# Normed x kept in DRAM, token-major operands copied once, bonus weights in the selector

## The chip, the cores and the metric

The kernel runs on one core of one Trainium2 chip. The metric is the device time of one execution in microseconds; for the kernel before, three runs gave a median of 797.93 us (796.2 to 800.12). A core has a matrix engine (PE), a vector engine (DVE), a scalar engine (ACT), a general engine (POOL) and an engine that issues most transfers (SP). PE writes into eight PSUM banks of 128 x 512 fp32; the other operands lie in SBUF.

## The reference

Two decoder layers over 512 tokens of width 1024. The change lies in layer 0, RWKV-7 time mixing:

```python
xn = rms_norm(h, norm_pre[0])
x_prev = pad(xn)[:, :-1]
xmix = xn + (x_prev - xn) * mu[c]          # one mix for each of r, k, v, g (and two more)
r, k, v, g = xmix[c] @ w_in[c]             # 1024 x 1024 each
decay = exp(-exp(-softplus(-w_pre) - 0.5)) # w_pre and a from two small products
kk = k * k_k / norm(k * k_k);  k = k * (1 + (a - 1) * k_a)
state = state * decay - (state @ kk) (kk * a)^T + v k^T;  y = state @ r      # over tokens
y = group_norm(y) * lnx_g + lnx_b
y = (y + sum(r * k * r_k, head) * v) * silu(g)
out = y @ w_out
```

Layer 1 is differential attention. Each layer ends with a gated embedding: p @ ple_w, gated by sigmoid(h @ ple_gate), normed and added.

## The kernel before, in words

All of layer 0 is built by about thirty Python generators, which a planner (`Streams`) runs against each other. Each yields the engine and an estimated duration of its next piece, waits for named events, or takes and frees buffers; the planner always records the piece that can start first by its estimates. So the order of every engine is a table that the planner makes from its estimated costs, and a changed cost, wait or buffer moves work far away. On the chip each engine goes through its order strictly, and an instruction that waits stops all behind it. SP's transfers are in one such queue.

Work is done in *dense groups*: three matmuls of 128 x 512 for one 128 x 128 block of weights, with operands split into a high and a low part (`mm3`, L285 to L287). `fill` (L907) runs the projections in the order r, k, v (first halves), r, k, v (second halves), the embedding's product `p` of layer 0, g, g, and the embedding of layer 1. Each half has 8 blocks of x times 4 output tiles, 32 groups. Its weights come through `w_load` (SP) and `w_split` (ACT, DVE, POOL), its operand, a mix of x with its neighbour token, through `mix` (L532). The first half of r, k and v forms the mixes (`mixed`, L512: ACT, DVE, ACT, DVE) and stores them in DRAM (mD, L529); the second half loads them again (L542). The mixes of g are formed ahead by `mix_ahead`, once the second half of k is done, and all halves of g load them.

Buffers are few: 43 ring slots of 4 KB per partition (R), 9 of 2 KB (H), and 8 PSUM banks (p), which projections and everything else share. xh, the normed and transposed x, holds four R slots until `mix_ahead` is done.

Between the dense groups runs the recurrence. `decay` (L740) forms decays and partial operands of one 128-wide tile from two small products (L749, L750). `k_evac` evacuates k and normalises it; its product r * k goes, scaled by r_k on ACT (L904), through `head_sums` with the selector `hsel` on PE (L824). `gram` (L984) forms products of keys within 128 tokens, `inverse` solves the triangular systems: a substitution on DVE, two sets of 64 small matmuls (L1087, L1101), and copies of small blocks. It begins with a load of identity blocks (L1025, `in_eye`), which ACT copies to PSUM (L1030). `operands` transposes keys into token-major form and copies them back into their place in four copies on ACT (L1152). `recur` goes through eight chunks of 64 tokens for each half of the heads: products with the Gram matrix (L1188), with the state (L1201), and the state's update (L1229 on PE, L1241 and L1244 on DVE). `finish` norms, adds the bonus, gates (L1310) and splits the result for the output projection (`layer_end`), whose groups follow `fill` directly. `pe_evac` copies the embedding's product to H on ACT (L1501) and SP stores it (peD, L1504); `v_evac` stores v (vcD, L664), and `operands` loads it (L1142).

## Time and profile before

| | |
|---|---|
| median of three runs | 797.93 us |
| profiled execution, its span | 797.09 us, 795.3 us |
| PE busy | 756.1 us (95%), 5016 matmuls |
| DVE, ACT, POOL busy | 589.8, 454.5, 201.9 us |
| mean granted clock of PE | 0.989 |
| moved by transfers | 148.79 MB, 187 GB/s |
| dense matmuls (L285 to L287) | 2400 |

In the prediction, a row of the page's fifth part or of a view by groups reads: line, engine, operation, output <- inputs, shapes, count | busy us, mean ns of one | idle us of the engine before them, and what ended it. A row of a timeline reads: start, length in us, engine, line, operation, count, and in brackets the idle time before it with its releaser. A row "PE p L749 <- ACT R L1115" tells how long the one waited for the other: total, times, longest. A row of a view by windows reads: window, its length, busy time and count of each engine (of PE alone where there is one), the granted clock, the share of the DMA engines, GB/s. A row of transfers ends with KB each and the median us from issue to landing.

### The profile page before, as it was taken

What the parts mean: (1) busy time and instruction counts of PE and PEld (TensorE: products, weight loads), DVE (VectorE), ACT (ScalarE), POOL (GpSimd) and SP (SyncE); (2) the same over time, 40 slices, a digit from 0 to 9 for tenths busy, and PEclk for the clock granted to TensorE, in tenths of its full rate; (3) what the DMA queues carried; (4) which work ended last, traced back from release to release, by engine and by line L of the source; (5) the groups of instructions that cost most, each with busy time, mean ns of one, the idle gap of its engine ahead of it and who ended that gap; (6) DMA issues with size and microseconds to landing.
All of it is one profiled execution on the core that took longest, in us unless ns stands there. A gap on an engine that the chain in (4) does not pass through costs nothing.

```text
span 795.3 us, 13941 instructions
## 1 busy us (share of the span) xinstructions
PE 756.1 (95%) x5016; PEld 605.1 (76%) x5016; DVE 589.8 (74%) x1360; ACT 454.5 (57%) x1078; POOL 201.9 (25%) x221
## 2 busy tenths in 40 slices
PE   6899999998999899999989999999999999999996
PEld 3576578875777677777778888887888888888884
DVE  2989999976798898998676685446874768835844
ACT  3779745688875446664444564333764566743431
POOL 2416615521451425666010010000000001100000
PEclk9999999998999899999999999999999999999998
DMA  8585669843684687463446444488943523314602
GB/s 325 197 285 196 245 225 290 298 147 105 209 286 171 217 301 258 145 228 105 133 166 247 133 146 135 172 309 226 312 158 92 159 53 121 117 43 159 259 6 106
DMA packets 66677, 148.79 MB, mean 187 GB/s; under 512 B 6576, under 2 KB 27312, under 8 KB 66608
## 3 DMA queue, kind: packets, MB, share of 16 engines
q1 hardware_dynamic: 43824, 112.25, 41.9%
q10 hardware_dynamic: 22784, 35.66, 13.1%
q8 instruction: 39, 0.64, 0.3%
q14 instruction: 30, 0.25, 0.1%
HBM read 110.13 MB, written 37.75 MB: 186 GB/s over the span
## 4 chain that ended last, share of the span: by engine, by line
PE 70%; DVE 8%; ACT 8%; DMA 8%; issue 2%; POOL 2%; SPq 1%; ACTq 0%; POOLq 0%; DVEq 0%
PE p L285 18%; PE p L287 18%; PE p L286 18%; PE p L1788 2%; PE p L984 2%; PE p L1188 2%; ACT R L270 1%; PE p L1753 1%; PE p L1752 1%; PE p L1201 1%; DMA R<-bD 1%; PE p L1779 1%; DMA RAW<-in_ple_w 1%; PE p L1410 1%; DMA R<-mD 1%
## 5 line engine op out<-in xcount | busy, mean ns | idle before, releaser
L285 PE MATMUL p<-R,R 128*128 128x512 f32 x800 | 326.4, 408 | 3.2 <-DVE R L270 1.7
L286 PE MATMUL p<-R,R 128*128 128x512 f32 x800 | 314.1, 393 | 3.8 <-DVE R L525 3.6
L287 PE MATMUL p<-R,R 128*128 128x512 f32 x800 | 314.4, 393 | 0.0
L285 PEld LDWEIGHTS p<-R,R 128*128 128x128 f32 x800 | 151.3, 189 | 37.1 <-DVE R L270 1.9
L287 PEld LDWEIGHTS p<-R,R 128*128 128x128 f32 x800 | 151.0, 189 | 33.2 <-DVE R L1318 0.4
L286 PEld LDWEIGHTS p<-R,R 128*128 128x128 f32 x800 | 151.5, 189 | 32.4 <-DVE R L525 4.9
L318 POOL TENSOR_TENSOR R<-RAW,R 128x512 fp32r<-128x512 f32 x59 | 78.6, 1339 | 163.3 <-ACT R L270 89.1
L270 ACT CAST R<-RAW 128x512 fp32r<-128x512 f32 x110 | 66.1, 619 | 26.7 <-DMA RAW<-in_w_g 10.0
L318 DVE TENSOR_TENSOR R<-RAW,R 128x512 fp32r<-128x512 f32 x81 | 56.8, 715 | 11.0 <-ACT R L270 10.2
L324 DVE SCALAR_TENSOR_TENSOR R<-RAW,vec,R 128x512 fp32r<-128x512 f32 x64 | 46.6, 748 | 13.9 <-ACT R L322 13.7
L322 ACT ACTIVATE R<-RAW,vec 128x512 fp32r<-128x512 f32 x64 | 44.6, 720 | 17.0 <-DMA RAW<-in_b_w_in 9.1
L1397 POOL TENSOR_TENSOR hr<-hm,half 128x1 f32<-128x1 f32 x16 | 10.4, 648 | 147.2 <-DVE hm L1395 147.2
L1757 DVE CUSTOM_DVE_ANT_0 p<-p,cmask 128x128 f32<-128x128 f32 (+3 forms) x64 | 30.3, 509 | 17.4 <-PE p L1753 17.3
L1764 ACT ACTIVATE H<-p,mx 128x128 f32<-128x128 f32 (+3 forms) x64 | 33.3, 526 | 15.7 <-DVE mx L1761 14.1
L281 POOL TENSOR_TENSOR orr<-orm,half 128x4 f32<-128x4 f32 x8 | 8.4, 1055 | 123.3 <-DVE orm L279 93.3
L1054 DVE TENSOR_TENSOR p<-p,H 128x126 f32<-128x126 f32 (+22 forms) x124 | 32.6, 263 | 4.3
L1051 DVE TENSOR_TENSOR H<-p,R 128x126 f32<-128x126 f32 (+22 forms) x124 | 30.5, 246 | 1.1
L1534 DVE SCALAR_TENSOR_TENSOR R<-H,R 128x512 f32<-128x512 f32 x16 | 11.1, 691 | 24.5 <-ACT H L1527 23.1
L1527 ACT ACTIVATE H<-p 128x512 f32<-128x512 f32 x16 | 9.5, 596 | 31.6 <-PE p L287 31.6
L521 DVE SCALAR_TENSOR_TENSOR p<-R,vec,p 128x511 f32<-128x511 f32 x32 | 23.5, 747 | 5.4 <-ACT p L519 5.3
L519 ACT ACTIVATE p<-R,omm 128x512 f32<-128x512 f32 x32 | 22.0, 695 | 5.0 <-DVE R L525 3.7
L1788 PEld LDWEIGHTS p<-R,H 128*128 128x128 f32 x160 | 22.1, 191 | 2.8 <-ACT H L1805 0.5
(227 smaller groups left out, 1249.4 us busy)
## 6 DMA issues: line engine op xcount, KB each, us to landing
R<-mD SPq DMA_DIRECT2D x40, 512.0 KB, 5.3
mD<-R ACTq DMA_DIRECT2D x32, 512.0 KB, 4.3
RAW<-in_ple_gate SPq DMA_DIRECT2D x16, 512.0 KB, 3.7
RAW<-in_kv_w SPq DMA_DIRECT2D x16, 512.0 KB, 3.9
RAW<-in_b_w_in SPq DMA_DIRECT2D x16, 512.0 KB, 3.9
R<-bD ACTq DMA_DIRECT2D x24, 256.0 KB, 5.2
R<-in_x SPq DMA_DIRECT2D x8, 512.0 KB, 6.8
RAW<-in_w_r SPq DMA_DIRECT2D x8, 512.0 KB, 4.0
```

Of the source, the lines that this page charges most:

```text
L270: (nc.scalar.copy if sc.eng == "ACT" else ENG[sc.eng].tensor_copy)(dst, src)
L285: nc.tensor.matmul(ps, ah, bh, start=first, stop=False)
L286: nc.tensor.matmul(ps, ah, bl, start=False, stop=False)
L287: nc.tensor.matmul(ps, al, bh, start=False, stop=last)
L318: ENG[sc.eng].tensor_sub(lo, f, hi.bitcast(F32))
L322: nc.scalar.activation(hi, f, AF.Copy, scale=g)
L324: nc.vector.scalar_tensor_tensor(lo, f, g, hi.bitcast(F32), ALU.mult, ALU.subtract)
L1051: ve.tensor_mul(tmp[:, 0:m, 0:w], bc(xs[:, s_ : s_ + 1, 0:w], [P, m, w]), bc(nb[:, s_ + 1 : 32, s_ : s_ + 1], [P, m, w]))
L1054: ve.tensor_add(xs[:, s_ + 1 : 32, 0:w], xs[:, s_ + 1 : 32, 0:w], tmp[:, 0:m, 0:w])
L1757: nc.vector.tensor_tensor_reduce(scs[m][:, 0:n], scs[m][:, 0:n], cmask[:, S - n : S], 1.0, -3.0e38, ALU.add, ALU.max, mx[:, m : m + 1])
L1764: nc.scalar.activation(E[m][:, 0:n], scs[m][:, 0:n], AF.Exp, bias=mx[:, m : m + 1], scale=0.125, accum_out=sm[:, m : m + 1])
L1788: nc.tensor.matmul(po[:, x * P : (x + 1) * P], aT[:, kb * P : (kb + 1) * P], vT[hg, kb // 2][:, kb % 2, x * P : (x + 1) * P], start=(kb == 0),
```

## The change

Five things are done:

1. `x_scale` stores each pair of normed x tiles to DRAM (xD, four stores of 512 KB on SP). When both parities have formed the first half of v's mixes and the stores are issued, `x_away` frees the four R slots. `mix_ahead` loads x from xD, 512 KB for two tiles, into an R slot, and waits for the third chunk of the recurrence instead of the second half of k.
2. `operands` takes a second R slot for each pair of chunks and copies the four transposes there in one ACT copy of 128 x 512, instead of four in place.
3. The bonus weights r_k are multiplied into eight selectors once (`bonus_maps`, one DVE instruction); the scaling of r * k on ACT is gone.
4. `recur` adds the state into the PSUM tile and multiplies the decay from there to SBUF. The copy of chunk-end decays (pcall) moves from ACT to POOL.
5. `finish` leaves the gated result in PSUM and splits it with ACT and DVE alone. The norm's gains are loaded after the fifth chunk instead of after the first inverse.

```diff
@@ x_scale
             yield "set", ("xh", d)
+            if d % 2:
+                yield "DMA!", 1.7
+                nc.sync.dma_start(xD[d // 2], xh[d // 2])
+                yield "set", ("stored", d // 2)
@@ mix_all, mix_ahead
             yield from mix(key, hf, par)
+            yield "set", ("mixes", par, key)
+
+    def x_away():
+        for par in range(2):
+            yield "wait", ("mixes", par, MIXES[2][0])
+        for n in range(4):
+            yield "wait", ("stored", n)
+        yield "free", "R", 4
...
-        yield "wait", ("dense", "k", 1)
-        for key in AHEAD:
-            for d in range(par, NT, 2):
-                yield "take", "R", 1, True
-                yield from mixed(key, d, R([P, 2, S], F32R))
-                yield "free", "R", 1
-        yield "free", "R", 2
+        yield "wait", ("rec", 2, 0)
+        for n in range(par, 4, 2):
+            yield "take", "R", 1, True
+            x = R([P, 2, S])
+            yield "DMA", 1.7
+            nc.sync.dma_start(x, xD[n])
+            for key in AHEAD:
+                for u in range(2):
+                    yield "take", "R", 1, True
+                    yield from mixed(key, 2 * n + u, R([P, 2, S], F32R), x[:, u])
+                    yield "free", "R", 1
+            yield "free", "R", 1
@@ decay
-        yield "ACT!", 0.1
-        nc.scalar.copy(pcall[:, :, i], pf[:, :, 64])
+        yield "Pool!", 0.1
+        nc.gpsimd.tensor_copy(pcall[:, :, i], pf[:, :, 64])
@@ head_sums, k_evac
+    def bonus_maps():
+        yield "wait", ("r", 0)
+        yield "DVE+", 0.4
+        nc.vector.tensor_mul(hselr, bc(hsel.unsqueeze(1), [P, NT, 32]), bc(rkvec.unsqueeze(2), [P, NT, 32]))
...
-            nc.tensor.matmul(pn[32 * q : 32 * q + 32], hsel, SQ[what, 4 * g + q], start=True, stop=True)
+            sel = hsel if what == "sq" else hselr[:, 4 * g + q, :]
+            nc.tensor.matmul(pn[32 * q : 32 * q + 32], sel, SQ[what, 4 * g + q], start=True, stop=True)
...
-        yield "ACT", 0.57
-        nc.scalar.activation(rk, rk, AF.Copy, scale=rkvec[:, i : i + 1])
@@ operands, recur
-                yield "take", "R", 1
-                UV[cq, g] = R([P, 2, S])
+                yield "take", "R", 2
+                UV[cq, g], BT[cq, g] = R([P, 2, S]), R([P, 2, S])
...
-            yield "ACT", 0.63
-            for ii in range(4):
-                nc.scalar.copy(bkt(4 * g + ii, cq, par), pt[:, ii * P : (ii + 1) * P])
+            yield "ACT", 0.5
+            nc.scalar.copy(BT[cq, g][:, par], pt)
...
-                        nc.vector.tensor_add(sv, sv, qv)
-                        qv = sv
-                    yield "DVE+!", 0.42
+                        nc.vector.tensor_add(qv, qv, sv)
+                    yield "DVE!", 0.42
                     nc.vector.tensor_mul(sv, qv, bc(pcall[hs, c_, 4 * g : 4 * g + 4].unsqueeze(2), [HN, 4, HN]))
@@ finish, gains_of_norm
-            nc.vector.scalar_tensor_tensor(w[:, xs], pt[:, xs], vcol(V_LB, 4 * g + x), gt[:, xs], ALU.add, ALU.mult)
-        yield "free", "pw", 1
+            nc.vector.scalar_tensor_tensor(pt[:, xs], pt[:, xs], vcol(V_LB, 4 * g + x), gt[:, xs], ALU.add, ALU.mult)
...
-        yield "ACT/DVE+", (0.52, 0.34)
-        copy(hi, w)
-        yield "Pool+/DVE+", (1.23, 0.6)
-        ENG[sc.eng].tensor_sub(lo, w, hi.bitcast(F32))
+        yield "ACT", 0.48
+        nc.scalar.copy(hi, pt)
+        yield "DVE", 0.6
+        nc.vector.tensor_sub(lo, pt, hi.bitcast(F32))
+        yield "free", "pw", 1
...
-        yield "wait", ("prep", 0, 0)
+        yield "wait", ("rec", 4, 0)
```

PE records the same matmuls as before, in another order among themselves. At three places the order is shown; numbers behind a tile's name rise in the order in which the planner took the tiles. Lines of the change are those of the new file, some 5 to 30 higher for the same code (L285 to L287 become L286 to L288).

First, ACT around the identity blocks of the fourth inverse (L1030 before, L1057 now), while the first embedding product is evacuated (L1501, now L1526). Before:

```order
L1501 COPY H_2936<-p_2919 128x512
L270 CAST R_2961<-RAW_2704 128x512
L1501 COPY H_2970<-p_2935 128x512
L1501 COPY H_2983<-p_2969 128x512
L1030 COPY p_3010<-H_2994 128x512
L270 COPY H_2993<-R_2877 32x128 x3
L270 COPY H_2993<-R_2878 32x128 x3
L1501 COPY H_3005<-p_2982 128x512
L1501 COPY H_3042<-p_3004 128x512
```

Now:

```order
L1526 COPY H_2946<-p_2907 128x512
L528 CAST R_2950<-p_2955 128x512
L271 CAST R_2953<-RAW_2832 128x512
L528 CAST R_2933<-p_2935 128x512
L271 CAST R_3007<-RAW_2832 128x512
...
L1057 COPY p_3078<-H_3060 128x512
L271 COPY H_3059<-R_2770 32x128 x4
L271 COPY H_3059<-R_2771 32x128 x3
L271 CAST R_3070<-RAW_3020 128x512
L271 CAST R_3116<-RAW_3020 128x512
```

The copy of the identity blocks stood ahead of the last two evacuations; now it stands behind the last of them (H_2946), and casts of gate weights (L271 from RAW) follow it.

Second, PE after the last matmuls of the second inverse (L1101 before, L1128 now) up to the next decay (L749 and L750, now L769 and L770). Before:

```order
L1101 MATMUL p_1988<-H_1781,H_1783 32x32
L1188 MATMUL p_1992<-R_1830,R_987 64x64 x2
...
L1201 MATMUL p_1992<-R_1716,R_447 128x128
...
L285 MATMUL p_1982<-R_1521,R_1795 128x512
...
L285 MATMUL p_2062<-R_1521,R_1795 128x512
...
L749 MATMUL p_2085<-R_274,R_1452 128x512
```

Now:

```order
L1128 MATMUL p_1969<-H_1777,H_1779 32x32
L1214 MATMUL p_1945<-H_1978,R_969 64x64 x2
...
L769 MATMUL p_2019<-R_278,R_1460 128x512
...
L286 MATMUL p_1495<-R_1672,R_1440 128x512
...
L286 MATMUL p_1502<-R_1672,R_1440 128x512
...
L286 MATMUL p_1478<-R_1710,R_1481 128x512
...
L286 MATMUL p_1487<-R_1710,R_1481 128x512
...
L286 MATMUL p_1495<-R_1710,R_1481 128x512
...
L769 MATMUL p_2076<-R_278,R_1460 128x512
```

A product with the Gram matrix, one with the state and two dense groups (the first matmul of each is shown) stood between; now it is a product, an earlier decay and five dense groups, and the state's product stands ahead of the inverse's matmuls.

Third, SP while v ends and the embedding begins. Before, and then now:

```order
L301 DMA RAW_2863<-in_w_g 128x1024
L1504 DMA peD<-H_2871 128x512
L664 DMA vcD<-H_2831 128x512
L1504 DMA peD<-H_2910 128x512
L1504 DMA peD<-H_2920 128x512
L1504 DMA peD<-H_2936 128x512
L301 DMA RAW_2975<-in_w_g 128x1024
```

```order
L572 DMA R_2725<-xD 128x1024
L302 DMA RAW_2750<-in_w_g 128x1024
L547 DMA R_2759<-mD 128x1024
L547 DMA R_2800<-mD 128x1024
L1529 DMA peD<-H_2810 128x512
L683 DMA vcD<-H_2768 128x512
L1529 DMA peD<-H_2823 128x512
L1529 DMA peD<-H_2840 128x512
L302 DMA RAW_2832<-in_w_g 128x1024
L683 DMA vcD<-H_2776 128x512
```

A load of x and two loads of kept mixes now stand right ahead of the embedding's stores (peD), and v's stores (vcD), some of which went out earlier, stand among them.

More of the change, by code (lines that the diff above doesn't have):

```diff
@@ L217, in yoco_kernel @@
     peD = dram.tile([2, NB, P, D], F32, name="peD")
+    xD = dram.tile([4, P, 2, S], F32, name="xD")
     mD = dram.tile([4, NT, P, 2, S], F32, name="mD")
@@ L510, in yoco_kernel, with mixed @@
     mixes = {}
-    def mixed(key, d, t):
+    def mixed(key, d, t, x):
         c = MIX[key]
@@ L518, in mixed @@
         yield "ACT", 0.57
-        nc.scalar.activation(m, x_at(d), AF.Copy, scale=omm[:, c, d : d + 1])
+        nc.scalar.activation(m, x, AF.Copy, scale=omm[:, c, d : d + 1])
         yield "DVE", 0.67
-        nc.vector.scalar_tensor_tensor(m[:, 1:], x_at(d)[:, 0 : S - 1], vcol(V_MU + c, d), m[:, 1:], ALU.mult, ALU.add)
+        nc.vector.scalar_tensor_tensor(m[:, 1:], x[:, 0 : S - 1], vcol(V_MU + c, d), m[:, 1:], ALU.mult, ALU.add)
         yield "ACT", 0.48
@@ L543, in mix @@
             else:
-                yield from mixed(key, d, t)
+                yield from mixed(key, d, t, x_at(d))
             yield "set", ("mix", key, hf, d)
@@ L694, in yoco_kernel @@
     rkvec = later("rkvec", [P, NT])
+    hselr = T(ax, [P, NT, 32], "hselr")
     der = T(ax, [P, 6, NT], "der")
@@ L922, in yoco_kernel @@
     sc.add(late_loads(), 1)
+    sc.add(bonus_maps(), 5)
     for g in range(2):
@@ L927, in yoco_kernel @@
         sc.add(mix_ahead(par), MIXP[2])
+    sc.add(x_away(), 0)
     sc.add(w_load(), WLP)
@@ L1120, in inverse @@
         yield "set", ("prep", g, cp)
-    def bkt(i, cq, par):
-        return BK[i][:, cq, 2 * par : 2 * par + 2, :].rearrange("p a j -> p (a j)")
+    BT = {}
     def operands(g):
@@ L1229, in recur @@
                     nc.tensor.matmul(
-                        pS[hs, cols(ii, hh)], bkt(4 * g + ii, cq, par)[:, hs], uv[:, cols(ii, hh)], start=True, stop=True
+                        pS[hs, cols(ii, hh)], BT[cq, g][:, par, cols(ii, hh)], uv[:, cols(ii, hh)], start=True, stop=True
                     )
@@ L1251, in recur @@
             if par == 1:
-                yield "free", "R", 3
+                yield "free", "R", 4
             yield "set", ("rec", c_, g)
```

3 lines of the change are left out of this document (2 added, 1 removed).

## The prediction

> **What bounds the kernel now.** I read the page first, then the waits of PE, then the windows of 20 us and of 2 us, and last the timeline around the two longest holes.
>
> ```profile
> span 795.3 us, 13941 instructions
> PE 756.1 (95%) x5016; PEld 605.1 (76%) x5016; DVE 589.8 (74%) x1360; ACT 454.5 (57%) x1078; POOL 201.9 (25%) x221
> ...
> 257.35 0.39 PE L285 MATMUL p<-R,R 128*128 128x512 f32 x1
> 257.58 0.39 PE L286 MATMUL p<-R,R 128*128 128x512 f32 x1
> ...
> PE p L1201 <- DVE R L1244: 1.6, 2, 0.8
> ```
>
> PE is busy for 756.1 of 795.3 us. The dense matmuls are shown 0.39 us long but start every 0.23 us (257.35, 257.58), one behind another; three of them make one group of 0.68 us. The change takes no matmul away: the 64 transposes, the sums of heads and the products are as many as before. So only the 39 us in which PE idles, and stretches in which it runs slowly, can be won, and every new idle time on PE costs its full length. Some of the 39 us lie ahead of the first matmul and behind the last, where the change does nothing. The rest lies in layer 0, and its two largest pieces come with a halved clock:
>
> ```profile
> 257.59 0.59 ACT L1501 COPY H<-p 128x512 f32<-128x512 f32 x1 [0.81 <-PE p L287]
> 263.02 0.59 ACT L1030 COPY p<-H 128x512 f32<-128x512 f32 x1 [4.84 <-DMA H<-in_eye]
> 266.03 2.08 PE L984 MATMUL p<-R,R 64*128 64x128 f32 x16 [3.12 <-ACT H L1501]
> ...
> 264.00:266.00 2.00, 0.00 (x0) 0.78 0.01 3
> 266.00:268.00 2.00, 1.97 (x16) 0.50 0.60 230
> 268.00:270.00 2.00, 2.00 (x7) 0.50 0.17 42
> 270.00:272.00 2.00, 2.00 (x6) 0.51 0.80 254
> ```
>
> **Hole A.** ACT stands for 4.84 us at the copy of the identity blocks of the fourth inverse (L1030), whose load has not landed. Behind it in ACT's queue are two evacuations of the first embedding product (L1501), which hold PSUM banks, and PE waits 3.12 us for one of these banks. Then the granted clock (in the four window rows the number behind the bracket) falls to a half. These rows lose 2 us times 0.22, 0.50, 0.50 and 0.49, which is 3.4 us; about 0.9 us of the idle time lies in them and was lost anyhow, at a half 0.4. Hole A costs 3.1 + 3.0 = 6.1 us.
>
> ```profile
> 179.39 1.20 PE L1101 MATMUL p<-H,H 32*32 32x32 f32 x64
> 180.52 0.69 PE L1188 MATMUL p<-R,R 128*64 128x64 f32 x16
> 181.13 1.16 PE L1201 MATMUL p<-R,R 128*128 128x128 f32 x8
> 185.48 0.50 PE L749 MATMUL p<-R,R 128*128 128x512 f32 x1 [1.81 <-ACT R L1115]
> 187.13 1.12 PE L1188 MATMUL p<-H,R 128*64 128x64 f32 x16 [0.48 <-DVE H L270]
> 189.61 0.79 PE L285 MATMUL p<-R,R 128*128 128x512 f32 x1 [1.35 <-DVE R L800]
> ...
> 180.21 3.35 ACT L270 COPY R<-H 32x128 f32<-32x128 f32 x11
> 183.57 2.14 ACT L1115 COPY R<-p 32x128 f32<-32x128 f32 x8
> ...
> 186.00:188.00 2.00, 1.52 (x21) 0.65 0.00 0
> 188.00:190.00 2.00, 0.65 (x7) 0.50 0.00 0
> 190.00:192.00 2.00, 2.00 (x6) 0.50 0.00 0
> 192.00:194.00 2.00, 2.00 (x17) 0.64 0.20 39
> ```
>
> **Hole B.** After the second inverse's last matmuls (L1101) ACT writes 11 + 8 small blocks, 5.5 us, before a bank comes free for a decay (L749). PE has 3.1 us of other work, then idles 1.81, 0.48 and 1.35 us, 3.6 in all. The clock is low in four rows: 0.70 + 1.00 + 1.00 + 0.72 = 3.4 us, less 0.9 for the idle time inside them, leaves 2.5. Hole B costs 6.1 us.
>
> A rule of the Trainium skill speaks against what I make of these halvings: "TensorE: Matmul & The Clock Gate", section "HAM oscillation — how this bites in real kernels", has the clock halve after a gap in PE's work of over about 3.4 us. Here it halved at a gap of 3.12 us, and once where no gap was over 1.81 us. By the rule these halvings aren't the holes' work and would stay: hole A would be worth 3.1 and hole B 3.6.
>
> **The change part by part.** Terms that are won are negative.
>
> *Fourth inverse's identity load (hole A).* In the new order of ACT all eight evacuations of the first embedding product stand ahead of that copy. Behind it stand casts of gate weights for the second half and copies for the inverse itself, whose result is wanted only some 65 groups later. The same wait there delays nothing that PE wants soon: -6.1 (bounds -6.1 and 0, should the evacuations wait for something else).
>
> *After the second inverse (hole B).* In PE's new order a product, a decay and five dense groups stand before the next decay: 0.6 + 0.45 + 5 x 0.68 = 4.5 us of cover where there were 3.1, against 5.5 us of small copies, of which the first 0.4 us ran before L1101 ended. That leaves 0.6 us of the 1.8. The waits behind it hang on the rest of ACT's queue, and this queue gets shorter:
>
> ```profile
> L1152 ACT COPY R<-p 128x128 f32<-128x128 f32 x64 | 12.2, 278 | 1.9 <-PE p L1149 1.8
> L904 ACT ACTIVATE H<-H,rkvec 128x512 f32<-128x512 f32 x8 | 5.8, 722 | 0.0
> L1501 ACT COPY H<-p 128x512 f32<-128x512 f32 x16 | 9.3, 588 | 10.9 <-PE p L287 9.0 <-issue 1.1 <-ACT H L682 0.6
> ```
>
> Removed are 12.2 + 5.8 = 18.0 us; sixteen copies of the form of L1501 come in, 9.4 us. ACT loses 8.6 us of work between the first transposes and the last, a good part of it here. But key evacuations and decays remain queued on it in the same stretch, and they are what PE waits for next. I take half of hole B: -3.0 (bounds -6.1 and 0).
>
> *State in PSUM.* The sum now overwrites the PSUM tile, and the decay is multiplied from PSUM.
>
> ```profile
> L1244 DVE TENSOR_TENSOR R<-R,pcall x24: 407/422/1280, 177.6 to 372.0; 64x256 f32<-64x256 f32 x24
> L1244 DVE TENSOR_TENSOR R<-p,pcall x4: 389/422/427, 166.8 to 308.4; 64x256 f32<-64x256 f32 x4
> ```
>
> From SBUF it takes up to 1280 ns, from PSUM never over 427. PE waited 1.6 us for L1244 in all. Half of it: -0.8 (bounds -1.6 and 0).
>
> *End of the last chunk.* The gated output stays in PSUM, its high part is made by ACT, its low part by DVE.
>
> ```profile
> 388.61 0.43 DVE L270 CAST R<-R 128x512 fp32r<-128x512 f32 x1
> 389.09 0.50 PE L285 MATMUL p<-R,R 128*128 128x512 f32 x1 [1.68 <-DVE R L270]
> ```
>
> Two dense groups (1.36 us) now stand between the last transposes and the matmuls that want them; ACT's cast is 0.15 longer than DVE's 0.43, and a hop between engines is added. -0.9 (bounds -1.7 and +0.5).
>
> *x to DRAM.* Four stores of 512 KB go onto SP's queue between weight loads. Each waits for its scaling on DVE (L504), and the loads behind it wait too.
>
> ```profile
> 37.92 1.80 DVE L504 SCALAR_TENSOR_TENSOR R<-R,vec,H 128x512 f32<-128x512 f32 x1
> ...
> 39.20 13.93 SPq L301 DMA_DIRECT2D RAW<-in_w_k  x4
> ...
> 51.62 0.40 PE L285 MATMUL p<-R,R 128*128 128x512 f32 x1
> ```
>
> The last scaling ends at 39.7, the first load of k's weights goes out at 39.2 and its first use is at 51.6. That cover hides it: 0 (without it a store's landing, 4.3 by the row below).
>
> *x back, and the gate's mixes.* A mix on ACT now waits for a load, where x lay in SBUF.
>
> ```profile
> R<-mD SPq DMA_DIRECT2D x11, 512.0 KB, 4.7
> ...
> DMA to landing us min/median/max: 2.6/4.8/9.9
> ...
> mD<-R ACTq DMA_DIRECT2D x32, 512.0 KB, 4.3
> ```
>
> Between the first load of x and its mix, PE's order holds a state product, two sets of key transposes, a product and two groups, about 5 us; loads of this size and place land in 4.7, at worst (all traffic of the kept mixes) 9.9. Queued behind the mix on ACT are a key norm's copy and the next transposes' evacuation, which PE reaches some 4 us later. +0.5 (bounds 0 and +1).
>
> *Recurrence of the second half of the heads.* PE's order now has fifteen groups between its fourth and fifth chunk and then five to six per chunk, where there were five to eight. Two more waits like the 0.8 of L1244: +1.6 (bounds 0 and +4).
>
> *Traffic between v and the gate.* The gate's mixes are formed later, so four of their stores (2 MB) now fall together with the embedding's eight and v's four stores (3 MB), three loads of gate weights (1.5 MB), one of x, two of mixes (1.5 MB) and small ones (0.5 MB): 8.5 MB in some thirty groups and two Gram steps, 22 us, or 390 GB/s.
>
> ```profile
> 220.00:240.00 20.00, 19.17 (x246) 15.07 (x245) 19.05 (x36) 13.13 (x33) 10.83 (x15) 1.00 0.88 305
> ```
>
> The fullest stretch near here moved 305 GB/s. Some of it will slip, and H buffers come free late: +2 (bounds 0 and +15, worked out below).
>
> *Selector product, copies of pcall on POOL, the later load of the norm's gains.* One DVE instruction in all; eight short ones on an engine with 25% busy; a load ahead of its use: 0, under 1 together if all were bare.
>
> Sum: -6.1 - 3.0 - 0.8 - 0.9 + 0.5 + 1.6 + 2 = -6.7. The profiled execution took 797.09 us, its span 795.3; the median of the three runs is 797.93, so the span becomes 788.6, the profiled time 790.4 and the median **791**.
>
> **The rivals.** *The holes move.* Order and lengths disagree elsewhere instead: PE waits as long at the first inverse's end or at the embedding's evacuations, with a halving each. For it speaks that hole A hangs on one load and hole B on one queue, and both are as long elsewhere; against it, that ACT has 8.6 us less to do. Holes A and B are won and paid back: 797.
>
> *DMA backlog, on the other side.* If the 8.5 MB run at 305 GB/s they take 28 us instead of 22. The embedding's evacuations then wait for H buffers by up to 5 us, with a halving (3). Later the gate's sixth mix is late too: between its store and its first matmul stand about 10 us of PE work, and in the crowded stretch around hole A store and load took
>
> ```profile
> R<-mD SPq DMA_DIRECT2D x10, 512.0 KB, 6.1
> ...
> mD<-R ACTq DMA_DIRECT2D x3, 512.0 KB, 7.4
> ```
>
> 13.5 us together: 4 us, and again a halving. 5 + 3 + 4 + 3 = 15 instead of the 2 above: -8.7 + 15 = +6.3, or 804. It decides from the point at which a kept mix's store and load together take longer than the 10 us of work between them. Against it: much of the traffic can slip into the 20 us that follow.
>
> *Halvings that the waits don't cause.* If the two low stretches of the clock come from something else, they stay, and 3.0 + 1.2 of the sum falls away: 795. The rule of the skill's page would have it so. Both stretches begin inside the holes, which speaks against it.
>
> *Ring slots that nobody uses* would leave only the last two wins: the order speaks against it, since v's last weights are now loaded ahead of the second pair of chunks, not behind the third. It ends with the first rival.
>
> **How the numbers follow.** Forecast 0.56, with its own range 784 to 794; holes that move 0.22; halvings that stay 0.05; backlog 0.17. A measurement of this kernel can tell 0.5%, 4 us, from no change: faster is below 793.9, slower above 801.9. The forecast is faster, the two middle cases are the same, the backlog is slower: 0.56, 0.27, 0.17. The range reaches from 783 (both holes won whole) to 804.
>
> **What would show it.** Hole A is gone if no wait of PE over 1 us ends on the embedding's evacuation and ACT's wait for in_eye comes after them. Hole B shows as waits of PE after L1128 (the second inverse) of 1.5 to 2 us in all and at most one halving. A granted clock of 1.00 in nearly all windows from 140 to 400 would show the forecast right; PE's busy time would be near 753 us. Wrong it is if peD stores land in over 6 us with PE waiting, if ACT waits more than 2 us for xD, or if the clock halves three times or more.

## The result and the profile after

| | kernel before | changed kernel |
|---|---|---|
| median of 19 runs each | 796.3 us (792.65 to 800.12) | 801.62 us (799.7 to 805.64) |
| ratio, 95% interval | | 1.0075 (1.006 to 1.009) |
| span of the profiled execution | 795.3 us | 798.1 us |
| mean granted clock in it | 0.989 | 0.993 |

The changed kernel is slower by 4.8 to 7.2 us. The forecast was 791 and faster; the time lies inside the range of 783 to 804, on its other side. That is luck: the upper end of the range came from a backlog of transfers, which the trace does not show. The profiled execution of the changed kernel took 799.88 us, close to its fastest, so its trace shows some 2.8 of the 5.3 us between the medians.

The page of the changed kernel begins:

```profile
span 798.1 us, 13883 instructions
...
PE 756.3 (95%) x5016; PEld 602.8 (76%) x5016; DVE 591.8 (74%) x1360; ACT 450.8 (56%) x1021; POOL 194.0 (24%) x223
```

PE is as busy as before (756.1) and idles 2.6 us more. ACT lost 3.7 us of work, not the 8.6 that were forecast. The waits of PE in the changed kernel (engine and line that waits, what ended the wait, us in total, times, longest; its lines are 1 to 27 higher than those of before, so L286 is the dense L285, L769 the decay L749, L1011 the Gram product L984, L1214 the product L1188):

```profile
PE p L769 <- DVE R L530: 3.4, 3, 1.8
PE p L1214 <- ACT H L271: 3.3, 3, 2.0
PE p L287 <- DVE R L530: 3.1, 3, 1.3
PE p L1011 <- ACT R L1178: 2.6, 1, 2.6
PE p L1255 <- ACT H L786: 2.1, 1, 2.1
PE p L1176 <- DVE R L1020: 1.7, 1, 1.7
...
PE p L286 <- ACT R L1340: 0.9, 1, 0.9
...
PE p L1227 <- DVE R L1269: 0.8, 2, 0.6
```

Three rows of the same view of the kernel before:

```profile
PE p L286 <- DVE R L525: 3.6, 3, 1.3
...
PE p L1410 <- DVE R L1469: 2.2, 1, 2.2
...
PE p L749 <- DVE R L525: 0.3, 1, 0.3
```

The totals of before over 1.5 us in layer 0, behind its first matmul, were 3.6, 3.1, 2.2, 1.8, 1.7, 1.6 and 1.6 us. The first, waits for the low part of a mix, is nearly the same now (L287 <- L530, 3.1). Two of the others are left, halved: the last chunk's (L286 <- ACT L1340) and the state's (L1227). Others have come; the decays' wait for a mix's low part was 0.3 us and is 3.4. Added up over the trace by stages, waits over 0.15 us and what the halved clock adds to the time between the starts of two matmuls (against the same pair of matmuls at full clock) are:

| stage (us) | before: waits + halved clock | after: waits + halved clock | difference |
|---|---|---|---|
| up to 160 | 6.5 + 0 | 10.8 + 1.3 | +5.7 |
| 160 to 260 | 5.0 + 2.3 | 5.5 + 0 | -1.9 |
| 260 to 300 | 4.7 + 2.8 | 2.6 + 1.7 | -3.3 |
| 300 to 400 | 3.9 + 0 | 6.2 + 0 | +2.4 |
| behind 400 | 3.6 + 0 | 1.0 + 0 | -2.7 |

These sum to +0.2. The first and the last matmul lie 2.5 us further apart than before; the other 2.3 us are spread over pieces too short to place (under 0.15 us each). Behind 400 us most of the gain is the 2.2 us of L1410, which no step of the prediction held.

The two stages for which the prediction promised a gain did gain, 5.2 us against 9.1. What it did not see is the stage ahead of 160 us. In the timeline of the changed kernel's PE there:

```profile
63.89 0.50 PE L769 MATMUL p<-R,R 128*128 128x512 f32 x1 [1.84 <-DVE R L530]
...
66.61 0.73 PE L769 MATMUL p<-R,R 128*128 128x512 f32 x1 [1.28 <-DVE R L530]
```

Four products of decays (L769, at 63.89, 64.60, 66.61 and 67.57 us) now stand behind the same dense group, while a mix's low part (L530) is late on VectorE; in the kernel before they started at 62.0, 64.8, 66.1 and 67.9 us. PE waits 1.84 and 1.28 us and the clock halves. The windows of the changed kernel (us, PE busy, granted clock, DMA share, GB/s) show both of its low stretches and the traffic around the second:

```profile
66.00:68.00 2.00, 1.39 (x4) 0.68 0.00 0
68.00:70.00 2.00, 2.00 (x6) 0.50 0.24 96
...
260.00:280.00 20.00, 18.54 (x116) 1.00 1.01 353
...
282.00:284.00 2.00, 2.00 (x8) 0.50 0.55 135
284.00:286.00 2.00, 2.00 (x8) 0.71 1.01 391
```

At the place of hole A, ACT's timeline in the changed kernel, and the row of PE that waits for it:

```profile
275.36 0.59 ACT L1057 COPY p<-H 128x512 f32<-128x512 f32 x1 [2.54 <-DMA H<-in_eye]
...
279.42 1.14 ACT L271 CAST R<-RAW 128x512 fp32r<-128x512 f32 x2 [1.40 <-DMA RAW<-in_w_g]
280.46 0.58 ACT L1178 COPY R<-p 128x512 f32<-128x512 f32 x1
```

```profile
281.10 1.51 PE L1011 MATMUL p<-R,R 64*128 64x128 f32 x14 [2.55 <-ACT R L1178]
```

No evacuation of the embedding product is behind the identity's load (L1057) any more, as forecast. But an operand copy (L1178) that frees a bank for the Gram products is, with a second wait in front of it, for gate weights.

### The profile page after: what moved, and what is told of

The parts are those of the page before. It is cut to its first block, busy times and chain, and to the rows that moved or that the text cites. A ratio compares the mean times of both kernels' runs of the same rounds, so it can differ in the third digit from the quotient of the medians.

```text
span 798.1 us, 13883 instructions
## 1 busy us (share of the span) xinstructions
PE 756.3 (95%) x5016; PEld 602.8 (76%) x5016; DVE 591.8 (74%) x1360; ACT 450.8 (56%) x1021; POOL 194.0 (24%) x223
## 4 chain that ended last, share of the span: by engine, by line
PE 62%; DVE 15%; ACT 8%; DMA 6%; issue 5%; POOL 3%; ACTq 0%; SPq 0%; POOLq 0%; DVEq 0%
PE p L286 16%; PE p L288 16%; PE p L287 16%; ACT R L271 2%; PE p L1813 2%; PE p L1214 2%; DVE R L319 2%; DMA RAW<-in_w_g 2%; DVE p L1081 1%; PE p L1778 1%; DVE R L530 1%; DVE H L1078 1%; PE p L1777 1%; DMA R<-bD 1%; PE p L1804 1%
## 5 line engine op out<-in xcount | busy, mean ns | idle before, releaser
L286 PE MATMUL p<-R,R 128*128 128x512 f32 x800 | 327.5, 409 | 2.5 <-ACT R L1340 0.9
L287 PE MATMUL p<-R,R 128*128 128x512 f32 x800 | 313.4, 392 | 3.3 <-DVE R L530 3.1
L288 PE MATMUL p<-R,R 128*128 128x512 f32 x800 | 314.0, 393 | 0.0
L286 PEld LDWEIGHTS p<-R,R 128*128 128x128 f32 x800 | 151.0, 189 | 36.6 <-ACT H L899 1.7
L288 PEld LDWEIGHTS p<-R,R 128*128 128x128 f32 x800 | 150.6, 188 | 33.3 <-DVE R L1342 0.4
L287 PEld LDWEIGHTS p<-R,R 128*128 128x128 f32 x800 | 151.3, 189 | 31.2 <-DVE R L530 4.2
L319 POOL TENSOR_TENSOR R<-RAW,R 128x512 fp32r<-128x512 f32 x49 | 64.8, 1328 | 150.3 <-ACT R L271 116.6
L319 DVE TENSOR_TENSOR R<-RAW,R 128x512 fp32r<-128x512 f32 x91 | 66.8, 748 | 14.5 <-ACT R L271 13.6
L271 ACT CAST R<-RAW 128x512 fp32r<-128x512 f32 x112 | 67.1, 617 | 15.3 <-DMA RAW<-in_w_g 4.5
L528 ACT CAST R<-p 128x512 fp32r<-128x512 f32 x32 | 18.6, 584 | 12.9 <-DVE p L526 12.5
L1481 ACT COPY R<-p 128x512 f32<-128x512 f32 x16 | 9.4, 589 | 26.3 <-PE p L288 26.2
```

What stands on the lines that cost most here:

```text
L271: (nc.scalar.copy if sc.eng == "ACT" else ENG[sc.eng].tensor_copy)(dst, src)
L286: nc.tensor.matmul(ps, ah, bh, start=first, stop=False)
L287: nc.tensor.matmul(ps, ah, bl, start=False, stop=False)
L288: nc.tensor.matmul(ps, al, bh, start=False, stop=last)
L319: ENG[sc.eng].tensor_sub(lo, f, hi.bitcast(F32))
```

## The experiments

Two theories were set against each other first. **Theory X**: keeping x in DRAM costs the time by its own work, its stores, loads and traffic. **Theory O**: the edits' work costs next to nothing, but any edit makes the planner write another order for every engine, and this order is worse. To tell them apart some kernels have their order *held*: the list of the planner's choices (which generator goes next and on which engine), taken from one kernel, stands in the other, and the planner follows it. What is edited then changes in place, and nothing else moves. The order in this sense takes in the engine that a piece goes to, which the planner chooses as well. The piece that does it:

```
 if best is None:
     who, self.only = HELD[self.at]      # next generator, its engine
     self.at += 1
     x = [y for y in self.st if y[6] == NAMES[who]][0]
```

The others are planned anew. Ratios are to the kernel before, run beside them.

### Which part, and whether by its work (e1 to e4)

**e1**: the order of before held; selector, pcall on POOL, state's sum in PSUM and the end of the last chunk edited in place.

```
-nc.scalar.activation(rk, rk, AF.Copy, scale=rkvec[:, i : i + 1])
+sel = hsel if what == "sq" else hselr[:, 4 * g + q, :]
-nc.vector.tensor_add(sv, sv, qv)
+nc.vector.tensor_add(qv, qv, sv)
```

> The kernel before, every engine's instructions in the order of before, with four of the edits made in place: bonus weights in the selector, pcall copies on POOL, the state's sum in PSUM, the end of the last chunk. Theory O (the loss comes from the new order that the planner wrote, not from the edits' own work): the four edits with the order held gain what the prediction gave the last two of them, 0.8 + 0.9, and up to 1.5 more since ACT loses 5.8 us: 792 to 796 where the kernel before takes 796. Theory X (keeping x in DRAM costs the time: stores and loads crowd the DMA engines, the gate's mixes come late): the same here, since x is not touched. A third possibility, that these edits lose themselves (the selector's product or POOL's port in the way): over 798.

Measured: 793.93 us, ratio 0.9993 (0.9966 to 1.0019). The four edits as work are worth something between -0.3 and +0.2%.

**e2**: the changed kernel's order held, the four stores of x left out; loads of the same size read the input x, so the gate's mixes are formed from x that is not normed.

```
-nc.sync.dma_start(xD[d // 2], xh[d // 2])
-nc.sync.dma_start(x, xD[n])
+nc.sync.dma_start(x, I["xT"][n])
```

> The changed kernel in its own order, but the four stores of the normed x are left out, and the later loads read the input x instead, of the same size (so the gate's mixes are formed from x that is not normed, and the output is another). Theory X: the trace after runs 3 to 4 us behind the trace before at the 48th dense group, with the DMA engines busier in 20 to 60 us; without the stores that goes, 797 to 799. Theory O: the delay there comes from a cast that the planner moved to VectorE and from the decays' new places; 801 to 802.5, within 1 us of the changed kernel.

Measured: 803.84 us, ratio 1.0106 (1.0066 to 1.0147): no faster than with the stores. Dense group 48, counted from zero, started at 70.7 us, where it stood at 72.0 with them and 68.3 before; the 1.3 us are the halved clock, which did not come at this place in this trace. The groups from the 104th on ran 0.9 to 2.5 us behind the changed kernel. So the stores are not it.

**e3**: the kernel before with the x part alone. **e4**: the changed kernel without it (x stays on the chip, the gate's mixes read it there). Both planned anew.

> The kernel before with the x part alone (stores, later loads, the gate's mixes formed late, the norm's gains later), planned anew. Theory X: slower than before by 5 us or more, 801 or over, with ACT waiting on in_eye or on gate weights near the last Gram products. Theory O: anywhere between 792 and 804, since the order is a third one; its time alone does not speak against O, but if its waits of PE are elsewhere than in the changed kernel it speaks for it.

> The changed kernel without the x part: x stays on the chip, the gate's mixes are formed early as before, the norm's gains load early, all other edits in, planned anew. Theory X: as fast as before or faster by what the other edits win, 790 to 796. Theory O: anywhere between 792 and 804; at 800 or over theory X falls, since the loss is there without x in DRAM.

Measured: e3 817.84 us, ratio 1.0273 (1.0227 to 1.0319); e4 794.07 us, ratio 0.9987 (0.9969 to 1.0006). By these two alone theory X has won: with the x part slow, without it not. But the same part costs 2.7% in one kernel and 0.9% in the other, and the waits in e3 are not those of the changed kernel: 6.7 us at the inverse and 4.8 us at a mix's load.

```profile
PE p L1107 <- DVE H L1095: 6.7, 1, 6.7
...
PE p L286 <- DMA R<-mD: 4.8, 1, 4.8
```

And e4 holds a longer hole A than the kernel before. Its ACT and its PE there:

```profile
267.17 0.59 ACT L1037 COPY p<-H 128x512 f32<-128x512 f32 x1 [7.30 <-DMA H<-in_eye]
```

```profile
270.27 0.80 PE L285 MATMUL p<-R,R 128*128 128x512 f32 x1 [6.60 <-ACT H L1506]
```

### Hole A, and the x part taken apart (e5 to e8)

**e5** and **e6**: the identity blocks are no longer loaded but written by ACT (a zero tile and two strided copies), e5 in the held order of e4, e6 in the held order of the changed kernel.

```
-nc.sync.dma_start(xs, I["eye32"])
-nc.scalar.copy(xs, eye)
+nc.scalar.activation(xf, bc(half[:, 0:1], [P, 512]), AF.Copy, scale=0.0)
+for w in range(2):
+    nc.scalar.copy(xf[:, 16 * w : 496 + 16 * w : 33], bc(dupm[:, w : w + 1], [P, 16]))
```

> The kernel without the x part (x on the chip, all other edits in), every engine's instructions in the order that it had, but the identity blocks of the inverses are no longer loaded: ACT writes a zero tile and two short strided copies of a constant in place of the copy from the load. In that order ACT stood 7.30 us for the load of the fourth inverse, PE 6.60 us, and the clock then halved. If the load is what holds hole A open: both go, 6.6 + 3, less about 1 that ACT's longer writing costs, so 785 to 788. If something behind it holds PE as long (the casts that wait for gate weights): 791 to 795.

> The changed kernel in its own order, with the same replacement of the identity's load. ACT stood 2.54 us for it and right behind it 1.40 us for a load of gate weights that took 9.0 us to land; the copy that PE wants comes after both. If traffic is what makes PE wait there (the weights' load): under 1 us is won, 800.5 to 802. If the identity's load alone: 2.5 and the halving's 2.1 are won, 796 to 798.

Measured: e5 788.6 us, ratio 0.9926 (0.99 to 0.9952), faster than both kernels and just outside the 785 to 788 of its first case; e6 800.76 us, ratio 1.0081 (1.0056 to 1.0105), no gain. In e4's order the load itself held the hole open. In the changed kernel's order the wait for gate weights behind it takes its place; in e6:

```profile
276.45 1.14 ACT L273 CAST R<-RAW 128x512 fp32r<-128x512 f32 x2 [1.93 <-DMA RAW<-in_w_g]
277.50 0.58 ACT L1183 COPY R<-p 128x512 f32<-128x512 f32 x1
```

PE's wait there fell to 1.0 us, and a wait of 1.5 us came up at the inverse and one of 1.7 at the last chunk's transposes (below).

**e7**: the changed kernel, each store of x a generator of its own, so that the scaling of the next tile is not planned behind it.

> The changed kernel, planned anew with each store of x as a stream of its own, so that in the planner's reckoning the scaling of the next tile of x no longer waits for the store's turn on the DMA queue. The work is the same. If the early loss (3 to 6 us behind the kernel before between the 48th and the 104th dense group, with a halving at 67 us) comes from that delayed scaling in the order: group 48 starts at 68 to 69 us and the time is 796 to 799. If it comes from the gate's late mixes and what they push: 800 to 804.

Measured: 800.08 us, ratio 1.0085 (1.0051 to 1.0119): no difference. It moved two rows of each engine's order at most, so it tested little.

**e8**: e4 with the gate's mixes held back until the event that the changed kernel waits for.

```
-yield "wait", ("dense", "k", 1)
+yield "wait", ("rec", 2, 0)
```

> The kernel without the x part (x on the chip, 794.07), with only the time of the gate's mixes changed, as late as in the changed kernel, planned anew. If the late mixes and their traffic beside the embedding's cost the time: 798 to 803, with waits of PE on gate weights, mixes or the identity's load between 255 and 310 us. If the cost lies in storing and reloading x: 792 to 796.

Measured: 793.54 us, ratio 0.9963 (0.9941 to 0.9984). This experiment says nothing on late mixes: no row of any engine's order differs from e4, presumably since ring slots already kept the mixes back that long. It is e4 a second time, and 0.9987 against 0.9963 shows how far two measurements of one order lie apart.

### What shifts the order, and by how much an order shifts the time (e9 to e12)

**e9**: the changed kernel, the stores as generators of their own and counted as nothing on the planner's DMA clock. **e10**: e4 with the four stores added and nothing read back. **e11**: the changed kernel without `x_away`, the four slots of x given back only behind the gate's mixes. Theory S: the reckoned time of the stores spoils the order; theory R: the slots given back early do.

> The changed kernel, work unchanged; each store of x is a stream of its own and counts nothing on the planner's single DMA clock (before: 1.7 us each, 6.8 us in all, ahead of the k weights). Theory S: the stores themselves cost nothing (the run without them, in the same order, was no faster), but their reckoned 6.8 us make the planner expect the k weights late and so it orders the first 150 us worse; with the reckoning gone PE's idle time in the first 150 us falls by some 3 of its 4.5 us over the kernel before, 796 to 798. Theory R (the four slots that x gives back early let the planner run other work ahead): no gain, 800 to 803.

> The kernel without the x part (794.07), with the four stores of x added and nothing else: x stays on the chip and is never read back. Theory S: this alone costs most of the loss, 798 to 802. Theory R: at most 1 us, 793 to 795.5.

> The changed kernel, x stored and read back as there, but the four ring slots of x are given back only when the gate's mixes are done, as in the kernel before. Theory R: what the early slots let run ahead is gone, 793 to 797. Theory S: the loss stays, 799 to 804.

Measured: e9 803.96 us, ratio 1.0102 (1.0073 to 1.013); e10 801.17 us, ratio 1.007 (1.0048 to 1.0091); e11 811.07 us, ratio 1.0197 (1.0169 to 1.0226). Theory S has e10 on its side and fails in e9; theory R fails in e10 and e11, and e11 lies above what either said. Neither stands. Whatever is touched, a time between 800 and 811 comes out.

**e12**: the kernel before, its work unchanged, one constant of the planner changed.

```
-PREF = 0.15
+PREF = 0.12
```

> The kernel before, work unchanged, with one constant of its planner changed (the advantage that an engine already chosen first has, 0.15 to 0.12 us), which moves some 200 rows on each of PE and VectorE. This gives the size of what an order alone does. If it is small (under 0.3%), the loss of the changed kernel needs a cause of its own; if it is 0.7% or more either way, the loss of 0.75% is within what any replanning does: 790 to 803.

Measured: 814.46 us, ratio 1.024 (1.0211 to 1.0269). This lies above the range that was expected. The same work in another order costs 18.6 us, more than three times the loss of the changed kernel. Some of it also went to other engines: VectorE has 1379 instructions where it had 1360, POOL 211 where it had 221. PE's waits in e12 are new ones once more:

```profile
PE p L824 <- DVE R L800: 4.5, 1, 4.5
PE p L1188 <- DVE H L270: 4.4, 2, 3.2
```

### The same work in two orders (e13 to e16)

**e13**: the changed kernel's edits with the identity written on the chip, so nearly the work of e6, on PE, VectorE, ACT and POOL in the order of e5. x is stored as in the changed kernel and read back in eight loads of 256 KB instead of four of 512 KB, each issued ahead of the mix before the one that needs it, the first at 183 us where e6's goes out at 198. What the gate's mixes wait for, the return of x's ring slots and the load of the norm's gains are those of e5.

```
 if d == par:
     xs = []
+for e in range(d if d == par else d + 2, min(d + 3, NT), 2):
+    xs.append(R([P, S]))
+    nc.sync.dma_start(xs[-1], xD[e // 2][:, e % 2])
```

> All of the changed kernel's edits, with x stored as there and read back in halves of 256 KB two mixes ahead, and the identity written on the chip, but on PE, VectorE, ACT and POOL the order of the kernel without the x part (e5, 788.6 us). Order theory: the x part's own work hides, 787 to 791. Work theory (reloads and their traffic cost the time): 796 or over, near the 800.8 of the same work in the changed kernel's order (e6).

Measured: 790.56 us, ratio 0.9926 (0.9902 to 0.9949). This is e5's ratio to the last figure: storing x and reading it back costs nothing beyond the 0.35%, 3 us, that the two intervals leave open. And e6, 1.0081, moves as many bytes (151.93 MB) and does nearly the same work in the order that the planner wrote for it. The order is 1.5%, some 10 to 12 us. No run tells the smaller and earlier loads of e13 apart from its order; but in the traces of e6 and of the changed kernel no engine waits for a load of x, so they leave little for the loads to win. The page of e6 begins, with PE's longest waits in layer 0 behind it:

```profile
span 799.0 us, 13875 instructions
...
PE 757.8 (95%) x5016; PEld 603.1 (75%) x5016; DVE 592.9 (74%) x1360; ACT 451.9 (57%) x1029; POOL 194.2 (24%) x223
```

```profile
PE p L772 <- DVE R L532: 3.4, 3, 1.5
PE p L1219 <- ACT H L273: 3.2, 3, 2.0
...
PE p L1260 <- ACT H L789: 2.1, 1, 2.1
PE p L1334 <- DVE R L1323: 1.7, 1, 1.7
```

The same of e13:

```profile
span 787.6 us, 13924 instructions
...
PE 754.6 (96%) x5016; PEld 604.0 (77%) x5016; DVE 585.2 (74%) x1352; ACT 450.8 (57%) x1031; POOL 203.8 (26%) x229
```

```profile
PE p L1207 <- DVE H L273: 2.1, 3, 1.2
PE p L1107 <- DVE H L1095: 1.6, 1, 1.6
```

PE idles 41.2 us in e6 and 33.0 us in e13, and is busy 3.2 us longer in e6. No one wait makes the difference; several of 1 to 2 us do, in e6 at decays (L772), products (L1219), state updates (L1260) and the last chunk's transposes (L1334).

**e14**: the kernel before in its own order, only the identity written on the chip. **e15**: e1 with the same.

> The kernel before in its own order, only the identity of the inverses written on the chip in place of its load. The prediction prices hole A at 6.1 us (3.1 of waiting, 3.0 of halved clock): 789 to 791. If the next thing in line (casts that wait for gate weights, the key matrices) takes its place: 793 to 796.

> The kernel of e1 (order of before, with the selector, POOL, PSUM and last-chunk edits) with the identity written on the chip. If the gains add: e1's 1 to 1.5 and hole A's 6.1, 788 to 790.

Measured: e14 794.49 us, ratio 0.9977 (0.9958 to 0.9996); e15 793.16 us, ratio 0.9964 (0.9948 to 0.998). Hole A is gone in both, and with it in e14 not 6.1 us but 1.8 (0.3 to 3.3); e15's gains do not add up to 788 to 790 either. PE at the fourth inverse, first in the kernel before, then in e14, and the windows of e14 there:

```profile
292.85 1.20 PE L1087 MATMUL p<-H,R 32*32 32x32 f32 x64 [1.61 <-DVE H L1075]
```

```profile
288.15 1.92 PE L1092 MATMUL p<-H,R 32*32 32x32 f32 x64 [4.06 <-DVE H L1080]
```

```profile
284.00:286.00 2.00, 0.09 (x1) 1.00 0.96 388
286.00:288.00 2.00, 0.00 (x0) 0.70 0.76 247
288.00:290.00 2.00, 1.85 (x65) 0.50 0.74 271
```

In the kernel before this wait was 1.61 us, from 291.2 on, with a full clock. PE now comes 7.1 us earlier (it runs dry at 284.1), VectorE lets it go on only 4.7 us earlier, and the difference is paid there, with a halved clock such as hole A had had.

**e16**: the changed kernel, work unchanged, with e12's constant.

> The changed kernel, work unchanged, with the planner's constant of e12 (0.15 to 0.12 us). Order theory: the time moves by several us either way, 792 to 815, and the waits of PE are at other places. Work theory: it stays within 2 us of 801.6, with the wait at the fourth batch's Gram product again.

Measured: 812.89 us, ratio 1.0208 (1.0174 to 1.0242), 11 us above the changed kernel for nothing but an order (and the engines that go with it). The wait at the Gram product is there again (2.2 us), but the largest is a new one:

```profile
PE p L1114 <- DVE H L1102: 7.9, 3, 7.3
```

### All times by order

| order | kernels in it (median us) |
|---|---|
| of before | before 796, e1 793.9, e14 794.5, e15 793.2 |
| of the changed kernel | changed 801.6, e2 803.8, e6 800.8; e7, two rows off, 800.1 |
| of e4 | e4 794.1, e8 793.5, e5 788.6, e13 790.6 |
| planned anew otherwise | e10 801.2, e9 804.0, e11 811.1, e16 812.9, e12 814.5, e3 817.8 |

Within one order the times differ by 3 to 6 us, the 6 by the identity's load; between orders by up to 24 us. Theory O stands, theory X falls: the x part does not cost time by its work. Why the planner's reckoning prefers worse orders once x goes to DRAM stays open; e9 to e11 take away two candidates, and no run takes one place of the order by itself.

The pages show one thing that the slow orders share. The planner chooses between VectorE and POOL for the low parts of split weights (L318, now L319), 140 instructions in every kernel. VectorE's row before and now:

```profile
L318 DVE TENSOR_TENSOR R<-RAW,R 128x512 fp32r<-128x512 f32 x81 | 56.8, 715 | 11.0 <-ACT R L270 10.2
```

```profile
L319 DVE TENSOR_TENSOR R<-RAW,R 128x512 fp32r<-128x512 f32 x91 | 66.8, 748 | 14.5 <-ACT R L271 13.6
```

The two fast orders, of before and of e4, give VectorE 81 and 83 of them; six of the seven slower orders (of the changed kernel, e3, e9, e10, e12 and e16) give it 87 to 91. The seventh, e11, is at 811 us with 83, so this alone does not decide. That it costs time is not shown: no run moves these instructions and holds the rest.

## Why the prediction was wrong, step by step

**Hole A, -6.1.** The order was read rightly (the embedding's evacuations do stand ahead of the copy), but the step "the same wait there delays nothing that PE wants soon" failed: an operand copy (L1178) stands behind it and behind the casts of gate weights. PE waited 2.55 us and lost 1.7 more by the clock; the stage 260 to 300 us gained 3.3. The size was wrong too: e14 closes the hole in the old order and wins 1.8 us, because a wait was priced as if the engine that is late next were on time. The fourth inverse's substitution on VectorE was 1.61 us late already, and that row was in the profile of before.

**Hole B, -3.0.** Right in its direction, two thirds of its size, and partly luck: the stage gained 1.9, by the clock (2.3) and not by the waits, which grew by 0.4. The longest are 0.76, 2.09 and 0.56 us where they were 1.81, 0.48 and 1.35, and the clock stays full. e14 makes even this gain doubtful. There hole B has its old waits (1.82, 0.48 and 1.80 us), and yet the clock stays at 1.00, as PE's timeline and the windows of e14 show:

```profile
184.33 0.50 PE L752 MATMUL p<-R,R 128*128 128x512 f32 x1 [1.82 <-ACT R L1120]
185.99 0.69 PE L1193 MATMUL p<-H,R 128*64 128x64 f32 x16 [0.48 <-DVE H L272]
188.47 0.50 PE L287 MATMUL p<-R,R 128*128 128x512 f32 x1 [1.80 <-DVE R L803]
```

```profile
184.00:188.00 4.00, 1.86 (x22) 1.00 0.00 0
188.00:192.00 4.00, 3.49 (x41) 1.00 0.18 44
```

e1 (1.77, 0.49 and 1.79 us) and e15 (1.78, 0.48 and 1.79) keep the full clock there too. So 2.5 of hole B's 6.1 us were a halving that these waits do not bring each time.

**State in PSUM, -0.8, and end of the last chunk, -0.9.** Both right: the multiplication never takes over 0.43 us now, and waits for it fell from 1.6 to 1.3 us (L1269: 0.8 at L1227, 0.5 at L1214); the wait at the end is 0.86 where it was 1.68. Held in the old order, these edits, the selector and POOL's copies gave 0.07%, which its interval cannot tell from nothing.

**x to DRAM, 0, and x back, +0.5.** Right by e2 and e13: nobody on PE waited for a load of x.

**Recurrence of the second half, +1.6.** The stage 300 to 400 us lost 2.4; with the 0.8 won at its end the recurrence lost 3.2. It lies within the bounds, but the waits are not on the state. They are on copies of 64 x 256 out of PSUM that the recurrence itself makes (L1214 <- ACT H L271); ahead of the longest, 2.01 us, ACT stood 2.02 us for POOL, which clears the tile that the copy writes:

```profile
332.21 0.75 ACT L271 COPY H<-p 64x256 f32<-64x256 f32 x2 [2.02 <-POOL H L1238]
```

**Traffic, +2.** The step's mechanism was there: 353 GB/s over 20 us, above the 305 that I had seen, and a load of gate weights, issued at 270.4, reached ACT's cast at 279.42. It is part of the wait at 281.1 and not more; the DMA backlog of the rivals, with late H buffers and late mixes, did not come.

**What no step held.** The stage up to 160 us lost 5.7 us. The prediction walked through the places that had been slow before and asked what becomes of them. It took for granted that the rest of the order would stay as good as it was; yet by a comparison of the two traces some 690 of PE's 5016 instructions and 370 of VectorE's 1360 stand at another place. The stage up to 160 us has one term in the sum, x to DRAM, at 0, and a new order as a whole has none. That is the step that failed: "only the 39 us in which PE idles ... can be won, and every new idle time on PE costs its full length" was written down, and only the first half was costed. e12 shows what the second half can weigh: 18 us. (The range suffered too: its lower end, 783, is said to be both holes won whole, but that gives 788, a sum of -9.8; 783 takes nearly every term at its lower bound, -15.5.)

The rival "the holes move" had the right mechanism with half the size: it gave back what was won, 797, and stopped there. "Halvings that the waits don't cause" is half right: in e14 one halving moved with its wait (from 265 to 287 us), so hole A's looks like the wait's work; hole B's was not tied to its waits alone. The rule of the Trainium skill ("TensorE: Matmul & The Clock Gate", section "HAM oscillation — how this bites in real kernels": a gap of over about 3.4 us halves the clock) takes in the 4.06 us of e14 by their length, though the clock fell there 2.7 us into the gap (0.70 in the window from 286 to 288 us). The clock also fell 2.2 us into the gap of 3.12 us before and just behind the one of 2.55 us in the changed kernel, and the rule would leave both of these out.

Of the signs named, these came: no long wait on the embedding's evacuation, no wait of ACT for xD. PE's busy time is 756.3, not 753, and the clock was low twice. Hole B's sign, waits of 1.5 to 2 us, did not come: they are 3.4 us. None of the three signs of being wrong came either (stores to peD with PE waiting, ACT waiting for xD, three halvings): they watched for the rivals that had been named, and none watched the stage up to 160 us.

## What to carry to other kernels

Where a planner, a scheduler or a pool decides the order, an edit is two changes, its work and a new order; hold the order and the first can be measured alone, change a constant that alters no work and the second can. Here four of the edits, held in the old order, measured 0.07%, the x part nothing beyond 0.35%, and a new order alone 2.4%; the single copy of the operands was never held by itself. So a new order should have been given a spread of its own, mostly on the slow side when the old order is a good one: of eight orders that the planner wrote anew, one was as fast as the old one and seven were 0.7 to 2.7% slower. Price a hole not at its length but at its length less the lateness of the next engine: in e14 VectorE was busy for 15.14 of the 16 us up to the fourth inverse and could not follow when PE came earlier.

The row of e14 on which the last sentence rests (window, then busy us of PE, weight loads, VectorE, ACT, POOL; clock, DMA share, GB/s):

```profile
272.00:288.00 16.00, 11.99 (x52) 9.42 (x51) 15.14 (x57) 4.67 (x8) 7.19 (x6) 0.96 0.94 333
```

## What was not expected of the hardware

The same waits in the same order halve the clock in one kernel and not in another: 1.81, 0.48 and 1.35 us did in the kernel before, 1.82, 0.48 and 1.80 us did not in e14. One trace of each kernel can't say how often a halving comes: over the 60 executions of the kernel before that ran beside the experiments, its mean clock went from 0.983 to 0.994, a difference of some 17 us at half the clock, with nothing changed. In the traces the clock falls and rises on a grid: low stretches ahead of the last matmul last 3.4 us (the changed kernel) or whole multiples of it (6.8 in the kernel before, 10.2 in e12, 13.7 in e16), and so do the full stretches between them. PE had idled for 1.81 and 2.21 of the 3.4 us ahead of the two falls of the kernel before, and for 1.87 and 2.55 ahead of the two of the changed kernel. That the place of this grid against the waits decides is likely, but not shown. A halved stretch cost less than half its length where PE waited in it: the two stretches of 6.8 us before, with 1.8 and 0.9 us of waits in them, cost 2.3 and 2.8 us. The DMA engines moved 353 GB/s over 20 us and 391 over 2 us at a share of 1.01, and loads of gate weights then landed in up to 9.0 us:

```profile
L302 SPq DMA_DIRECT2D RAW<-in_w_g x6: 333/354/1391, 256.6 to 286.2; - x6
...
DMA to landing us min/median/max: 3.5/4.7/9.0
```
